# Gathers tied behind the gate products, an output product in split passes, and a softmax scaled late

## The chip, the cores and the metric

One core of a Trainium2 chip runs the whole program. The metric is device time in microseconds (us) of one execution, as the median over runs. The engines are TensorE (PE, matrix products and transposes), VectorE (DVE), ScalarE (ACT) and GpSimd (POOL); SyncE (SP) issues most of the loads. Each takes its instructions in order and waits on semaphores for the others.

## The reference

Four sub-layers on x of 512 tokens by 1024 channels, each with an RMS norm ahead of it, a shift, scale and gate from a conditioning vector (`ada`), and a residual:

```
y = rglru_block(h)              # layer 0: h @ w_in, a causal convolution of width 4, two gates,
                                # a linear recurrence over time, (gelu(gate) * hs) @ w_out
x = x + g1 * y;  x = x + g2 * peer(h)
y = mla_block(h, k, v)          # layer 1: 16 heads of softmax(q k) v, then @ w_o
x = x + g1 * y;  x = x + g2 * peer(h)

def peer(h):                    # per token: 8 heads, 16 experts each of 16384
    s = scores of two halves of the query against 128 sub-keys each; top 16 of both, top 16 of the 256 sums
    idx = e1 * 128 + e2;  g = softmax(top scores)
    act = gelu(h . u_tab[idx]);  return sum of g * act * v_tab[idx]
```

## The kernel before

Activations are channels on partitions by 512 tokens. Most products are split: an fp32 operand becomes a rounded high part (`hi`, ScalarE) and the rest (`lo`, VectorE, L163), and `mm3` (L187 to L189) makes three passes, hi x lo, lo x hi and hi x hi, into one PSUM bank. `outer` (L207) instead multiplies fp32 operands in one matmul. Weights come as `raw`, `wtile` splits them into `whi` and `wlo`.

A scheduler orders the instructions of each engine by its own estimate of when they can run; the source only sets priorities. `tc.issue_after(x)` is a hand on it: the instructions of its block stand behind x on the engine of x, with no wait added. The program has five stages by time: the recurrent block (0 to about 205 us), `peer` of layer 0 (to about 1522), attention (to about 1845), `peer` of layer 1 (to about 3158), a final norm.

The recurrent block (L335 to L454) makes the norm column `rcol` (L244), normalises and splits eight chunks, adds up the `rec` products, convolves them on VectorE (`xc`, L379), makes `gate` and the two recurrence gates, scans (L433), multiplies by the gelu (L436) and goes through `w_out` (`wo`, L207) in a loop over k, the last two k per output chunk. Products of the conditioning vector with a column block of its weight (`adas`, L151, one VectorE instruction of 128x1024 each) are strewn among it.

Attention (L537 to L725) takes the heads one by one: `scores` makes the products `s`, the mask and the maximum, the exponential (ScalarE, sums beside it), the reciprocal of the sums (L660) and four scalings of `p` (L662). `turn` transposes `p` on TensorE (`tp`, L670) and splits it, `context` multiplies with the values (`pv`) and copies the result into `ot`.

`peer` (L851 to L1090) serves three of the four token blocks (384 tokens) densely and the last by gathers. Dense: for every group of experts, `u_part` multiplies hidden states with a split `u` weight (24 matmuls 128x384), and the gate values are written out (`gact`, through `gscr`). In the gate stage 24 `gate_group`s (L821) build the weights of all experts for 16 tokens each: VectorE makes the one-hots `oo` (L835) and the products `pr` (L837) in two halves, TensorE multiplies them (`wps`, L843), ScalarE copies, a DMA writes `wscr`. `et` (L808) are transposed expert numbers, ready after decoding `e` (L800). Thirteen `u_part`s (`UDEC`) stand ahead of the groups, others between them, `UEND` = 5 behind the last. Then the value pass: 128 steps t, each 18 matmuls `acc` of `al`/`ah` with `vh`/`vl`; a step's weights `wt` are read back from `wscr` (`wfirst` serves t = 0 and 1).

The gathers (`gather_steps`, L1103) are 256 steps a layer: GpSimd issues an indirect DMA of 128 rows (`grow`, 512 KB, four buffers, L1113), then VectorE makes a dot product with `hn` (L1117, `gdot`) for u or adds the scaled row into `gacc` (L1122) for v, in turns of 16. How many steps are given out by when is counted by `done`: four in the loop over `UDEC`, 94 (`EARLY`) by the second last gate group, the others over the value pass.

Of the kernel before, what the change touches and what calls it, by code (L numbers as in the profile page):

```python
# [15 lines left out]
AF = mybir.ActivationFunctionType  # L16
OP = mybir.AluOpType
# [4 lines left out]
P = 128  # L22
D = 1024
KC = D // P
T = 512
# [21 lines left out]
UEND = 5  # L47
FIRST = 4
EARLY = 94
# [32 lines left out]
class Trunk:  # L82
# [157 lines left out]
    def rstd_row(self, n):  # L240
# [3 lines left out]
        nc.vector.reciprocal(col[:, 1], col[:, 0])  # L244
# [90 lines left out]
    def rglru(self):  # L335
        nc, io, tc = self.nc, self.io, self.tc
        with tc.tile_pool(name="lru", bufs=52) as pool, ExitStack() as st:
# [11 lines left out]
            with tc.tile_pool(name="ada", bufs=1) as early:  # L349
                ws, h = [], []  # L350
                for k in range(KC):
# [7 lines left out]
                    if k == 0:  # L359
                        outs = [self.bank("rec") for _ in range(KC)]  # L360
                    if k < KC - 2:
                        self.outer3(outs, ws, h, [k])
            late = st.enter_context(tc.tile_pool(name="lru2", bufs=10))
            s2, s4 = self.softplus_neg()
            hba, hbx = self.half_bias("ba"), self.half_bias("bx")
            xc, rec = [], []
            for m in range(KC):
# [6 lines left out]
                                     bias=self.vec("conv_b", m))  # L374
            win = [self.wtile(io["w_in"][m], KC, eng=nc.vector) for m in range(2)]
            for m in range(KC):
                a = xc[m]
                for s in range(1, 4):
                    nc.vector.scalar_tensor_tensor(a[:, s:], rec[m][:, :T - s], self.vec("conv_w", (3 - s) * KC + m),  # L379
                                                   a[:, s:], op0=OP.mult, op1=OP.add)  # L380
# [36 lines left out]
            for hd in range(4):  # L417
# [12 lines left out]
                for j in js:  # L430
# [8 lines left out]
                    ys.append(tt[j])  # L439
            self.todo = [*range(16, 40), *range(96, 112), *range(40, 96)]  # L440
            self.adas(12, late)
# [4 lines left out]
            for k in range(KC):  # L446
                ws.append(self.wraw(io["w_out"][k]))
                if k < KC - 2:
                    self.outer(outs, ws, ys, [k])
            self.preload(AF.Sqrt, last_gelu)  # L450
            for m in range(KC):
                self.outer(outs, ws, ys, range(KC - 2, KC), m)
# [84 lines left out]
    def mla(self):  # L537
        nc, io, tc = self.nc, self.io, self.tc
        with tc.tile_pool(name="mla", bufs=12) as pool, ExitStack() as st:
# [87 lines left out]
            att, ots, qts, pns, pts = [], {}, {}, {}, {}  # L627
# [17 lines left out]
            def scores(hd):  # L645
# [15 lines left out]
                for b, p in enumerate(pns[hd]):  # L661
                    nc.vector.tensor_scalar(p, p, st[:, 3, b:b + 1], None, op0=OP.mult)  # L662
# [12 lines left out]
            def context(hd):  # L675
                hp, s = divmod(hd, 2)
                if s == 0:
                    ots[hp] = pool.tile([P, T], F32, name="ot", tag="t")
                ops = self.bank("pv")
# [4 lines left out]
                nc.scalar.activation(ots[hp][64 * s:64 * s + 64], ops[:64], AF.Copy)  # L684
# [136 lines left out]
    def gate_group(self, pool, l, b, sg, et, gp):  # L821
# [5 lines left out]
        for t0 in range(0, TG, HT):  # L827
# [9 lines left out]
            nc.vector.tensor_tensor(pr.rearrange("p (q a) e t -> p q a e t", q=2), oo[:, 0:n4].unsqueeze(1).to_broadcast(two),  # L837
# [390 lines left out]
```

## Time and profile before

| | |
|---|---|
| median of 3 runs | 3173.54 us (3168.76 to 3174.25) |
| profiled execution | 3173.62 us, span 3171.8 us |
| mean granted clock of TensorE | 0.975 of full speed |
| busy: PE, DVE, ACT, POOL | 95%, 82%, 43%, 27% of the span |
| DMA | 821.13 MB, mean 259 GB/s |

The span is the profiled part of the execution. A row of a view of lines gives an engine, an operation with output and inputs, its shape, busy time, mean duration and what ended the idle time before it. TensorE is pipelined: one matmul's duration is longer than the distance between two starts. [...]

### The profile page before, as it was taken

Reading aid. Unit: us, or ns where it says so; the run is one execution under the profiler, and the core shown is the slowest. Engines: PE = TensorE matmul, PEld = TensorE weight load, DVE = VectorE, ACT = ScalarE, POOL = GpSimd, SP = SyncE. Lnnn points to the kernel's source line nnn. Section 1 sums busy time; section 2 is a strip of 40 time slices with the busy share of each in tenths; the row PEclk is TensorE's granted clock in tenths of the full one; section 3 lists DMA queues with packets and bytes.
Section 4 is the critical chain, followed back from the end, with each engine's and each line's share of the span. In section 5 each row is a group of like instructions: output and inputs, shape, how many; then the busy total and the mean of one; then the engine's idle time right before and its main releaser. Section 6 shows DMA issues by size and latency. Waiting matters only on the chain.

```text
span 3171.8 us, 43218 instructions
## 1 busy us (share of the span) xinstructions
PE 2997.4 (95%) x15334; PEld 2626.9 (83%) x15334; DVE 2585.5 (82%) x4927; ACT 1377.0 (43%) x1960; POOL 860.7 (27%) x653
## 2 busy tenths in 40 slices
PE   6999997999899999999889989989899899999997
PEld 5659997999777889998667679989899688889996
DVE  8859999988788888888578868998987677777886
ACT  5533245655334333333555642445555233333333
POOL 0000015433132214443356500034432211134440
PEclk9999998999999999999899999999999899999999
DMA  7444578999999999998113244478999999999994
GB/s 290 149 160 140 173 241 307 335 316 317 308 346 347 367 330 328 333 342 285 42 45 106 78 145 137 145 279 304 337 321 314 293 320 303 321 313 331 341 325 142
DMA packets 345111, 821.13 MB, mean 259 GB/s; under 512 B 33600, under 2 KB 179136, under 8 KB 338496
## 3 DMA queue, kind: packets, MB, share of 16 engines
q1 hardware_dynamic: 239632, 460.91, 43.5%
q0 software_dynamic: 73728, 268.47, 23.8%
q10 hardware_dynamic: 31536, 89.00, 7.4%
q8 instruction: 121, 1.98, 0.2%
q14 instruction: 94, 0.77, 0.1%
HBM read 730.98 MB, written 87.29 MB: 258 GB/s over the span
## 4 chain that ended last, share of the span: by engine, by line
PE 74%; DVE 11%; issue 6%; DMA 5%; ACT 2%; POOL 2%; DVEq 0%; SPq 0%; POOLq 0%; ACTq 0%
PE acc L187 10%; PE acc L188 10%; PE acc L189 10%; PE u L187 9%; PE u L188 9%; PE u L189 9%; PE wps L843 5%; PE pq L187 2%; PE pq L188 2%; PE pq L189 2%; DVE wlo L163 1%; PE wo L207 1%; DMA ada_raw<-in_adaw_dram 1%; DMA grow<-in_u_dram,idx 1%; DVE grow L1117 1%
## 5 line engine op out<-in xcount | busy, mean ns | idle before, releaser
L1113 POOL DMA_INDIRECT grow<-in_u_dram,idx x256 | 341.3, 1333 | 1317.3 <-DVE oh L791 702.8
L187 PE MATMUL u<-hh,wlo 128*128 128x384 f32 x2048 | 690.6, 337 | 1.6 <-DVE wlo L163 1.6
L189 PE MATMUL u<-hh,whi 128*128 128x384 f32 x2048 | 687.4, 336 | 0.0
L188 PE MATMUL u<-hl,whi 128*128 128x384 f32 x2048 | 685.7, 335 | 0.0
L187 PE MATMUL acc<-vh,al 128*128 128x512 f32 x1536 | 573.7, 392 | 33.4 <-DVE al L163 30.6
L188 PE MATMUL acc<-vl,ah 128*128 128x512 f32 x1536 | 601.4, 392 | 1.2 <-DVE vl L163 1.2
L189 PE MATMUL acc<-vh,ah 128*128 128x512 f32 x1536 | 601.2, 391 | 0.0
L1113 POOL DMA_INDIRECT grow<-in_v_dram,idx x256 | 352.4, 1376 | 750.5 <-DVE gacc L1122 439.8
L163 DVE TENSOR_TENSOR wlo<-raw,whi 128x1024 fp32r<-128x1024 f32 x307 | 373.1, 1216 | 110.9 <-ACT whi L162 110.7
L163 DVE TENSOR_TENSOR vl<-vraw,vh 128x1024 fp32r<-128x1024 f32 x256 | 313.2, 1223 | 165.5 <-ACT vh L162 164.8
L162 ACT ACTIVATE whi<-raw 128x1024 fp32r<-128x1024 f32 (+2 forms) x364 | 349.5, 961 | 104.5 <-PE acc L189 29.1
L187 PEld LDWEIGHTS u<-hh,wlo 128*128 128x128 f32 x2048 | 385.8, 188 | 5.2 <-issue 1.5
L188 PEld LDWEIGHTS u<-hl,whi 128*128 128x128 f32 x2048 | 385.1, 188 | 2.8
L189 PEld LDWEIGHTS u<-hh,whi 128*128 128x128 f32 x2048 | 384.8, 188 | 0.0
L187 PEld LDWEIGHTS acc<-vh,al 128*128 128x128 f32 x1536 | 289.5, 189 | 96.7 <-issue 23.8
L188 PEld LDWEIGHTS acc<-vl,ah 128*128 128x128 f32 x1536 | 289.9, 189 | 60.6 <-DVE vl L163 1.6
L189 PEld LDWEIGHTS acc<-vh,ah 128*128 128x128 f32 x1536 | 289.7, 189 | 60.7
L162 ACT ACTIVATE ah<-gact 128x384 fp32r<-128x384 f32 x240 | 125.9, 525 | 481.0 <-PE acc L189 282.3
L1122 DVE SCALAR_TENSOR_TENSOR gacc<-grow,gdot,gacc 128x1024 f32<-128x1024 f32 x254 | 324.8, 1279 | 9.8 <-DMA grow<-in_v_dram,idx 8.5
L1117 DVE CUSTOM_DVE_ANT_0 grow<-grow,hn 128x1024 f32<-128x1024 f32 x256 | 309.1, 1219 | 25.8 <-DMA grow<-in_u_dram,idx 25.6
L162 ACT ACTIVATE vh<-vraw 128x1024 fp32r<-128x1024 f32 x256 | 268.8, 1051 | 131.4 <-DMA vraw<-in_v_dram 48.9
L843 PE MATMUL wps<-pr,oo 128*128 128x128 f16 x1536 | 190.5, 297 | 31.8 <-DVE pr L837 31.8
(337 smaller groups left out, 4175.4 us busy)
## 6 DMA issues: line engine op xcount, KB each, us to landing
raw<-in_uT_dram SPq DMA_DIRECT2D x256, 512.0 KB, 5.4
vraw<-in_v_dram SPq DMA_DIRECT2D x256, 512.0 KB, 6.0
ada_raw<-in_adaw_dram SPq DMA_DIRECT2D x112, 512.0 KB, 4.5
wscr<-stg ACTq DMA_DIRECT2D x48, 1024.0 KB, 6.2
wt<-wscr SPq DMA_DIRECT2D x32, 1536.0 KB, 13.1
gscr<-gsp ACTq DMA_DIRECT2D x152, 192.0 KB, 4.9
gact<-gscr SPq DMA_DIRECT2D x152, 192.0 KB, 6.1
raw<-in_w_pq_dram SPq DMA_DIRECT2D x32, 512.0 KB, 3.6
```

Source lines behind the costliest of these rows:

```text
L162: nc.scalar.activation(hi, src, AF.Copy)
L163: return (eng or nc.vector).tensor_tensor(lo, src, hi.bitcast(F32), op=OP.subtract)
L187: nc.tensor.matmul(out, al, bh, start=first, stop=False)
L188: nc.tensor.matmul(out, ah, bl, start=False, stop=False)
L189: return nc.tensor.matmul(out, ah, bh, start=False, stop=last)
L207: self.nc.tensor.matmul(outs[m], ws[k][:, m, :], acts[k], start=k == 0, stop=k == KC - 1)
L843: last = nc.tensor.matmul(wps[:, t * P:t * P + P], oo[:, n4 + a, :, t], pr[:, q * n4 + a, :, t], start=q == 0, stop=q == 1)
L1113: nc.gpsimd.indirect_dma_start(out=row, out_offset=None, in_=tabs[s], in_offset=bass.IndirectOffsetOnAxis(ap=idx[:, k:k + 1], axis=0))
L1117: nc.vector.tensor_tensor_reduce(row, row, hn, op0=OP.mult, op1=OP.add, scale=1.0, scalar=0.0, accum_out=col)
L1122: nc.vector.scalar_tensor_tensor(acc, row, col, acc, op0=OP.mult, op1=OP.add)
```

## The change

It has four parts, and line numbers of the lines behind move by up to 14 (`pr` L850, dot products L1131, `gacc` L1136).

In `peer`, no gather steps are given out in the loop over `UDEC`. In the gate stage the steps of a turn are placed under `issue_after` of the last `pr` product of the group before, `EARLY` is 90 instead of 94, and it is reached by the group that is fourth from the end (`QUIET`) instead of second. `UEND` is 7: two more `u_part`s stand behind the last group.

In the recurrent block, `w_out` and the activations `ys` are split and `outer3` makes three passes (192 matmuls) in place of 64 fp32 ones. All but the first chunk's step and the softplus stand behind the norm's reciprocal; the first twelve `adas` stand behind the last convolution.

In attention the four scalings of `p` go. The reciprocals are transposed on TensorE into a bank `rr` (four transposes a head), and `ot` is multiplied by it after the copy.

```diff
@@ -44,9 +44,9 @@
-UEND = 5
-FIRST = 4
-EARLY = 94
+UEND = 7
+QUIET = 4
+EARLY = 90
@@ -241,7 +241,7 @@
-        nc.vector.reciprocal(col[:, 1], col[:, 0])
+        self.recip = nc.vector.reciprocal(col[:, 1], col[:, 0]).ins
@@ -348,7 +348,7 @@
-                for k in range(KC):
+                def step(k):
@@ -356,12 +356,16 @@
-                    if k == 0:
-                        outs = [self.bank("rec") for _ in range(KC)]
...
+                        if not outs:
+                            outs.extend(self.bank("rec") for _ in range(KC))
...
+
+                outs = []
+                for k in range(KC):
+                    with tc.issue_after(self.recip) if k else ExitStack():
+                        step(k)
...
-            s2, s4 = self.softplus_neg()
@@ -372,12 +376,14 @@
+            with tc.issue_after(self.recip):
+                s2, s4 = self.softplus_neg()
...
-                    nc.vector.scalar_tensor_tensor(a[:, s:], rec[m][:, :T - s], self.vec("conv_w", (3 - s) * KC + m),
-                                                   a[:, s:], op0=OP.mult, op1=OP.add)
+                    conv = nc.vector.scalar_tensor_tensor(a[:, s:], rec[m][:, :T - s], self.vec("conv_w", (3 - s) * KC + m),
+                                                          a[:, s:], op0=OP.mult, op1=OP.add).ins
@@ -436,20 +442,22 @@
-                    ys.append(tt[j])
+                    ys.append(self.pair(pool, "y"))
+                    self.split(ys[j][0], ys[j][1], tt[j])
...
-            self.adas(12, late)
+            with tc.issue_after(conv):
+                self.adas(12, late)
...
-                ws.append(self.wraw(io["w_out"][k]))
+                ws.append(self.wtile(io["w_out"][k], KC, eng=nc.vector))
...
-                    self.outer(outs, ws, ys, [k])
+                    self.outer3(outs, ws, ys, [k])
...
-                self.outer(outs, ws, ys, range(KC - 2, KC), m)
+                self.outer3(outs, ws, ys, range(KC - 2, KC), m)
@@ -624,7 +632,7 @@
-            att, ots, qts, pns, pts = [], {}, {}, {}, {}
+            att, ots, qts, pns, pts, norms = [], {}, {}, {}, {}, {}
@@ -658,8 +666,7 @@
-                for b, p in enumerate(pns[hd]):
-                    nc.vector.tensor_scalar(p, p, st[:, 3, b:b + 1], None, op0=OP.mult)
+                norms[hd] = st
@@ -676,12 +683,18 @@
+                rr = self.bank("rr")
+                st = norms.pop(hd)
+                for b in range(NB):
+                    nc.tensor.transpose(rr[:64, b * P:b * P + P], st[:, 3, b:b + 1].to_broadcast([P, 64]), self.ident)
...
-                nc.scalar.activation(ots[hp][64 * s:64 * s + 64], ops[:64], AF.Copy)
+                o = ots[hp][64 * s:64 * s + 64]
+                nc.scalar.activation(o, ops[:64], AF.Copy)
+                nc.vector.tensor_tensor(o, o, rr[:64], op=OP.mult)
@@ -834,8 +847,9 @@
-            nc.vector.tensor_tensor(pr.rearrange("p (q a) e t -> p q a e t", q=2), oo[:, 0:n4].unsqueeze(1).to_broadcast(two),
-                                    toks(gp).rearrange("p (q a) e t -> p q a e t", q=2), op=OP.mult)
+            prod = nc.vector.tensor_tensor(pr.rearrange("p (q a) e t -> p q a e t", q=2),
+                                           oo[:, 0:n4].unsqueeze(1).to_broadcast(two),
+                                           toks(gp).rearrange("p (q a) e t -> p q a e t", q=2), op=OP.mult)
@@ -846,7 +860,7 @@
-        return last.ins
+        return last.ins, prod.ins
@@ -957,24 +971,24 @@
-                    while done < FIRST * (i + 1) // UDEC:
-                        next(gsteps)
-                        done += 1
...
-                wlast = [None, None]
+                wlast, plast = [None, None], []
...
-                    wlast.append(self.gate_group(pool, l, i // nsg, i % nsg, *prep[i // nsg]))
+                    w, p = self.gate_group(pool, l, i // nsg, i % nsg, *prep[i // nsg])
+                    wlast.append(w)
+                    plast.append(p)
...
-                    while done < min(EARLY, FIRST + (EARLY - FIRST) * (i + 1) // (nt - 2)):
-                        next(gsteps)
-                        done += 1
+                    with tc.issue_after(plast[max(0, i - 1)]):
+                        while done < min(EARLY, EARLY * (i + 1) // (nt - QUIET)):
+                            next(gsteps)
+                            done += 1
```

Ahead of the first gate product, DVE, layer 0 (`gdot<-grow,hn` is a gather's dot product, `oo` and `pr` belong to the first gate group). Before:

```order
L835 TENSOR_TENSOR oo<-iota_e,et 128x2048 x2
L817 CAST gp<-gt 128x16x8
L780 TENSOR_REDUCE gsum<-g 128x8
L798 TENSOR_TENSOR oh<-oh 128x4x128
L1117 ISA grow,gdot<-grow,hn 128x1024
L1117 ISA gdot 128x1
L818 TENSOR_TENSOR gp<-gt,gp 128x16x8
L781 RECIPROCAL gsum<-gsum 128x8
L1117 ISA grow,gdot<-grow,hn 128x1024
L1117 ISA gdot 128x1
L798 TENSOR_TENSOR oh<-oh 128x4x64
L837 TENSOR_TENSOR pr<-oo,gp 128x2048 x2
```

With the change:

```order
L848 TENSOR_TENSOR oo<-iota_e,et 128x2048 x2
L813 TENSOR_TENSOR e_4610<-oh 128x64
L830 CAST gp<-gt 128x16x8
L793 TENSOR_REDUCE gsum<-g 128x8
L163 TENSOR_TENSOR wlo<-raw,whi 128x1024
L804 TENSOR_TENSOR oh<-iota_m,rc 128x1024
L831 TENSOR_TENSOR gp<-gt,gp 128x16x8
L794 RECIPROCAL gsum<-gsum 128x8
L808 TENSOR_TENSOR oh<-oh,ib 128x1024
L850 TENSOR_TENSOR pr<-oo,gp 128x2048 x2
L1131 ISA grow,gdot<-grow,hn 128x1024
L1131 ISA gdot 128x1
```

No dot product is left ahead of the first `pr`; the layer's first stands right behind it.

Start of the value pass, DVE, layer 0 (`gacc` are gathers of v, `al` the first step's weights, `x<-x,wt` the first product with weights that are read back). Before:

```order
L151 ISA ada_junk,mod<-ada_raw,csil,vecs 128x1024
L151 ISA mod 128x1
L1122 SCALAR_TENSOR_TENSOR gacc<-grow,gdot,gacc 128x1024 x2
L998 TENSOR_TENSOR x<-x,wfirst 128x384 x2
L1122 SCALAR_TENSOR_TENSOR gacc<-grow,gdot,gacc 128x1024 x2
L163 TENSOR_TENSOR al<-x,ah 128x384 x2
L151 ISA ada_junk,mod<-ada_raw,csil,vecs 128x1024
L151 ISA mod 128x1
L1122 SCALAR_TENSOR_TENSOR gacc<-grow,gdot,gacc 128x1024
L471 CAST ps_a<-ps_pi 128x512
```

With the change:

```order
L1012 TENSOR_TENSOR x<-x,wfirst 128x384 x2
L151 ISA ada_junk,mod<-ada_raw,csil,vecs 128x1024
L151 ISA mod 128x1
L163 TENSOR_TENSOR vl<-vraw,vh 128x1024
L1136 SCALAR_TENSOR_TENSOR gacc<-grow,gdot,gacc 128x1024 x4
L151 ISA ada_junk,mod<-ada_raw,csil,vecs 128x1024
L151 ISA mod 128x1
L163 TENSOR_TENSOR al<-x,ah 128x384 x2
L1136 SCALAR_TENSOR_TENSOR gacc<-grow,gdot,gacc 128x1024 x4
L163 TENSOR_TENSOR vl<-vraw,vh 128x1024
L1012 TENSOR_TENSOR x<-x,wt 128x384 x3
L163 TENSOR_TENSOR al<-x,ah 128x384 x2
```

Four gathers stand ahead of the first `al` in one piece and four more behind it, ahead of the `wt` product, where one stood.

End of the recurrent block, DVE (`tanh<-tanh,gate` are the activations that go into `w_out`, `yl` their low parts, `wlo` the low parts of its rows among others, `x<-wo` the residuals). Before:

```order
L151 ISA mod 128x1
L436 TENSOR_TENSOR tanh<-tanh,gate 128x512
L433 SCALAR_TENSOR_TENSOR tanh<-a,tanh 128x512
L151 ISA ada_junk,mod<-ada_raw,csil,vecs 128x1024
L151 ISA mod 128x1
L436 TENSOR_TENSOR tanh<-tanh,gate 128x512
L278 SCALAR_TENSOR_TENSOR gs_f_1370<-mod,vecs 128x8
L163 TENSOR_TENSOR wlo<-raw,whi 128x1024
L282 SCALAR_TENSOR_TENSOR x<-wo,mod,x 128x512
L163 TENSOR_TENSOR wlo<-raw,whi 128x1024
L282 SCALAR_TENSOR_TENSOR x<-wo,mod,x 128x512
L163 TENSOR_TENSOR wlo<-raw,whi 128x1024
```

With the change:

```order
L439 SCALAR_TENSOR_TENSOR tanh<-a,tanh 128x512
L438 TENSOR_TENSOR tanh<-tanh,g 128x512
L163 TENSOR_TENSOR wlo<-raw,whi 128x1024
L163 TENSOR_TENSOR yl<-tanh,yh 128x512
L442 TENSOR_TENSOR tanh<-tanh,gate 128x512
L163 TENSOR_TENSOR yl<-tanh,yh 128x512
L439 SCALAR_TENSOR_TENSOR tanh<-a,tanh 128x512
L163 TENSOR_TENSOR yl<-tanh,yh 128x512
L442 TENSOR_TENSOR tanh<-tanh,gate 128x512
L163 TENSOR_TENSOR yl<-tanh,yh 128x512
L163 TENSOR_TENSOR wlo<-raw,whi 128x1024 x2
L282 SCALAR_TENSOR_TENSOR x<-wo,mod,x 128x512 x3
```

The last products of `w_out` wait for `yl` and `wlo` rows, which before were not there for `w_out`; the residual follows them.

## Rows read from the trace of the kernel before

**Rows 1.** The waits of TensorE over the span, from the line that waits to the line waited for: total us, times, longest us.

```profile
PE wps L843 <- DVE pr L837: 31.8, 8, 9.9
PE tp L670 <- DVE p L662: 13.9, 12, 3.0
PE et L808 <- DMA raw<-in_uT_dram: 8.0, 1, 8.0
PE gate L187 <- DVE wlo L163: 5.8, 1, 5.8
PE et L808 <- DVE e L800: 2.4, 1, 2.4
```

**Rows 2.** Timeline of TensorE, 483 to 503 us: start, duration, instruction, [idle before it <- what ended it].

```profile
492.50 0.48 PE L808 MATMUL et<-ident,e 128*128 128x128 f32 x1 [8.01 <-DMA raw<-in_uT_dram]
502.15 1.10 PE L843 MATMUL wps<-pr,oo 128*128 128x128 f16 x8 [8.96 <-DVE pr L837]
```

**Rows 3.** Timeline of VectorE, 470 to 504 us, same columns.

```profile
492.23 0.21 DVE L800 TENSOR_TENSOR e<-oh 128x64 f32<-128x64 bf16 x1
499.57 1.18 DVE L1117 CUSTOM_DVE_ANT_0 grow<-grow,hn 128x1024 f32<-128x1024 f32 x1
500.88 2.35 DVE L837 TENSOR_TENSOR pr<-oo,gp 128x2048 f16<-128x2048 f16 x2
```

**Rows 4.** The table of stretches behind four pauses: stretch, its length, busy time of PE, PEld, DVE, ACT and POOL (instructions), granted clock, DMA share, GB/s.

```profile
502.00:505.60 3.60, 3.45 (x30) 3.45 (x30) 3.60 (x8) 2.30 (x3) 1.52 (x2) 0.51 0.82 251
2136.50:2140.60 4.10, 4.04 (x33) 4.04 (x33) 4.01 (x8) 2.88 (x3) 0.94 (x1) 0.51 0.57 192
2242.90:2249.70 6.80, 3.07 (x27) 3.07 (x28) 6.80 (x13) 1.92 (x3) 3.24 (x3) 0.50 1.02 339
608.00:611.40 3.40, 3.40 (x26) 3.40 (x24) 3.40 (x5) 3.40 (x4) 0.87 (x1) 0.50 1.08 399
```

**Rows 5.** Waits of VectorE for gathered rows of u in two stretches, 440 to 830 us (layer 0) and 2080 to 2490 us (layer 1): total us, times, longest.

```profile
DVE grow L1117 <- DMA grow<-in_u_dram,idx: 6.3, 4, 3.8
DVE grow L1117 <- DMA grow<-in_u_dram,idx: 5.0, 5, 3.6
```

**Rows 6.** The list of DMA issues, 2215 to 2250 us: count, median us from issue to landing.

```profile
grow<-in_u_dram,idx POOLq DMA_INDIRECT x12, 8.0
```

**Rows 7.** Timelines at the start of the value pass of layer 1: TensorE, SyncE's queue, VectorE.

```profile
2468.68 0.76 PE L187 MATMUL acc<-vh,al 128*128 128x512 f32 x1 [10.20 <-DVE al L163]
2464.22 8.25 SPq L993 DMA_DIRECT2D wt<-wscr  x2
2478.35 1.03 DVE L998 TENSOR_TENSOR x<-x,wt 128x384 f32<-128x384 f32 x2 [9.30 <-DMA wt<-wscr]
```

**Rows 8.** The table of stretches, two pieces of the value passes of layers 0 and 1, columns as in rows 4.

```profile
950.00:1050.00 100.00, 97.86 (x428) 79.69 (x427) 81.25 (x112) 38.80 (x52) 24.75 (x17) 1.00 1.01 353
2500.00:2600.00 100.00, 100.00 (x443) 82.82 (x442) 74.63 (x106) 35.41 (x48) 14.99 (x16) 1.00 0.92 306
```

**Rows 9.** Timeline of VectorE among the convolutions, a `wlo` and an ada product.

```profile
79.94 1.22 DVE L163 TENSOR_TENSOR wlo<-raw,whi 128x1024 fp32r<-128x1024 f32 x1
82.39 1.27 DVE L151 CUSTOM_DVE_ANT_0 ada_junk<-ada_raw,csil,vecs 128x1024 bf16<-128x1024 f32 x1
```

**Rows 10.** TensorE by lines, 140 to 210 us (busy us, mean ns | idle before), and its timeline at the end of the recurrent product (first and last of 21).

```profile
L207 PE MATMUL wo<-tanh,raw 128*128 128x512 f32 x128 | 55.1, 592 | 0.0
65.04 0.39 PE L187 MATMUL rec<-hmh,wlo 128*128 128x512 f32 x1
69.58 0.39 PE L189 MATMUL rec<-hmh,whi 128*128 128x512 f32 x1
```

**Rows 11.** The table of stretches for 80 to 200 us, columns as in rows 4.

```profile
80.00:200.00 120.00, 118.79 (x351) 67.98 (x352) 89.95 (x138) 57.61 (x79) 0.00 (x0) 0.98 0.49 162
```

**Rows 12.** Attention: the scalings by lines over 1594 to 1846 us, timelines of VectorE, GpSimd and TensorE, and a stretch behind a pause (columns as in rows 4).

```profile
L662 DVE TENSOR_SCALAR p<-p,st 128x512 f32<-128x512 f32 x64 | 51.5, 864 | 0.5
1703.03 3.49 DVE L662 TENSOR_SCALAR p<-p,st 128x512 f32<-128x512 f32 x4
1715.02 1.76 DVE L662 TENSOR_SCALAR p<-p,st 128x512 f32<-128x512 f32 x3
1704.39 1.45 POOL L163 TENSOR_TENSOR qt<-qf,qt 96x512 fp32r<-96x512 f32 x1
1616.20 1.03 PE L670 MATMUL tp<-ident,p 128*128 128x128 f32 x8
1703.60:1710.40 6.80, 6.51 (x19) 5.28 (x20) 5.19 (x11) 1.57 (x3) 4.38 (x4) 0.50 0.15 48
```

**Rows 13.** Timeline of GpSimd, issues of gathered rows, 499 to 612 us: the first and the last of 29, and two between.

```profile
499.61 1.95 POOL L1113 DMA_INDIRECT grow<-in_v_dram,idx  x1 [2.40 <-DVE gp L818]
...
534.05 4.48 POOL L1113 DMA_INDIRECT grow<-in_v_dram,idx  x1 [5.79 <-DVE gacc L1122]
539.18 0.94 POOL L1113 DMA_INDIRECT grow<-in_v_dram,idx  x1 [0.65 <-DVE oh L798]
...
610.53 1.88 POOL L1113 DMA_INDIRECT grow<-in_u_dram,idx  x1 [4.21 <-DVE g L782]
```

**Rows 14.** Timeline of VectorE, 533.5 to 541 us.

```profile
540.61 1.22 DVE L835 TENSOR_TENSOR oo<-iota_e,et 128x2048 f16<-128x2048 f16 x1 [1.49 <-PE wps L843]
```

**Rows 15.** The gate products of layer 0, one tile's view: count, shortest, median and longest ns, first and last start.

```profile
L843 PE MATMUL wps<-pr,oo x768: 278/298/305, 502.1 to 799.4; 128*128 128x128 f16 x192
```

## The prediction

> **What bounds the kernel now.** I read the waits of TensorE first: TensorE is busy for most of the span, so what it waits for is what an edit can give back. Five of its waits are touched by the change [rows 1]: 31.8 us before the gate products `wps` for `pr`, 8.0 and 2.4 us before the transposes `et`, 13.9 us before the attention transposes `tp` for the scaled `p`, 5.8 us before a `gate` product of the recurrent block. Next I read the timeline at the largest of them. In layer 0 TensorE stands 8.01 us before `et` and 8.96 us before the first `wps` [rows 2]. VectorE shows who is late: `e` comes at 492.23, `pr` begins at 500.88, and gather rows' dot products of 1.18 us stand between [rows 3]. The first pause is put down to a DMA, but `et` starts as `e` ends, so VectorE is what TensorE waits for. The order of VectorE has 15 such dot products ahead of the first `pr` in either layer. [...]
>
> **The gate groups.** The change puts every dot product behind the `pr` of the group before; the new order has none ahead of the first `pr`. Fifteen at 1.18 us are 18 us of VectorE, about the two pauses of layer 0 (8.01 + 8.96 = 17.0) and more than layer 1's (2.4 + 9.9 = 12.3). I take these 29.3 us as gone; what is left of the list, 42.2 − 29.3 = 12.9 us, lies at later groups and has the same cause, `pr` behind dot products, so I count it too. [...] Together 49.2 us.
>
> Against it stands the tie itself. VectorE is in order, so a row that is not there when its turn comes holds `wlo`, `oo` and `pr` behind it, and TensorE after them. Today such waits are 6.3 us in layer 0 and 5.0 in layer 1 [rows 5]. The rows used to have a head start of 15 ahead of the first group and now have none; groups 2 to 5 carry 16 dot products instead of 10. Four row buffers are refilled in rounds of an issue on GpSimd, a landing of 8.0 us [rows 6] and a dot product. No row shows the new waits. Below, they are zero, or even negative by today's 11.3 us; above, they are what the first rival prices. I double today's: −11.3 us. The gates then give 49.2 − 11.3 = 38 us (range 14 to 49). Two `u` parts more behind the last group are work moved, not added: 48 matmuls on TensorE either way, and their loads move with them.
>
> **The start of the value pass.** In layer 1 TensorE waits 10.20 us for the first `al`, and then t = 2 needs `wt`, which is issued at 2464.22 and read at 2478.35 after a wait of 9.30 us [rows 7]. The issue follows the write of the last `u` part's activations, so more parts behind the last group do not bring it forward. What the first pause gives up, the second takes: zero, with the 10 us of one pause as a bound upward. In the new order the same path has ten to twelve gathers between the last `pr` and the first `al`, and three or four more ahead of the first `wt` product; a late round of rows there is the bound downward, −10 us.
>
> In the value pass eleven gathers more are left (80 done at its start, not 91), and by t = 84 eight of them are caught up. In layer 0 the DMA engines are full there (share 1.01 at 353 GB/s), in layer 1 not (0.92) [rows 8]. Eight rows of 0.52 MB at 353 GB/s are 11.9 us of transfer in layer 0 alone; TensorE was at 97.9 us of 100 in that stretch, so most of a small surplus is hidden. I take −3 us (0 to −12).
>
> **The recurrent block.** Three things pull forward. The first normalised chunk loses one ada product (1.27 us) and one `wlo` (1.22 us) ahead of it [rows 9]: 2.5 us. The pause of 5.8 us before the second gate product falls by the ada products that stood between the convolutions, two at 1.27 us: 2.5 us. The output product is 55.1 us for 128 records of 64 fp32 matmuls; three split passes are 192 matmuls at the pitch of the recurrent product, 21 of them from 65.04 to 69.58, 20 pitches, 0.227 us each [rows 10]: 43.6 us, so 11.5 less. The sum is 16.5 us, if TensorE alone counted. But VectorE has only 30.0 us idle of the 120 from 80 to 200 us (89.95 busy) [rows 11], and the change puts into it eight `wlo` at 1.22, eight `yl` (half the width, so 0.7 at most) and twelve ada products at 1.27 that used to lie earlier: 9.8 + 5.6 + 15.2 = 30.6 us. That fills it. The last `yl` then comes near 180 to 195 us with the output passes of the last chunks behind it, and TensorE waits for most of what it saved. I take 5 us; bounds −3 (VectorE late by its overflow and a wait more) and +16.5. Eight more ScalarE copies lie beside, ScalarE being busy half of that stretch (57.61 of 120).
>
> **Attention.** Out go 64 scalings with a mean of 0.864 us, 51.5 us of VectorE in all [rows 12], and the 13.9 us that TensorE waits for them; the transposes then wait for the exponential, a step earlier. In come 64 small transposes on TensorE: eight `tp` take 1.03 us, so 64 x 0.129 = 8.2 us, all on the path, and 16 products of 64x512, the size class of the scaling: 14 us of VectorE at most, 0.7 of them at the tail behind the last head. One of the half-clock stretches starts after such a wait, with 6.51 us of work [rows 12]; I take back 3. So 13.9 − 8.2 − 0.7 + 3 = 8 us (0 to 16).
>
> Among these rows four scalings take 3.49 us beside a GpSimd split, three take 1.76 with GpSimd idle: 0.87 against 0.59 each. [...]
>
> **Sum.** 38 + 0 − 3 + 5 + 8 = 48 us. The profiled execution took 3173.62 us (span 3171.8), the median is 3173.54, so 3173.6 − 48 = **3126 us**. About 0.2%, 6 us, is what a measurement of this kernel can tell from no change.
>
> **Rivals.**
>
> *Rows come late in the first groups* (chance 0.18). For: from 499.61 to 610.53 GpSimd issues 29 rows, one per 3.96 us, and one issue takes 4.48 us where another takes 0.94 [rows 13]; the long one lies under unbroken VectorE work, the short one in a pause of 1.49 us [rows 14]. VectorE gets fuller, so long issues become common. The 24 groups' products run from 502.1 to 799.4 [rows 15]. Two `u` parts leave this stretch, 48 matmuls of 384 columns, an estimate of 8.2 us at three quarters of 0.227 each; (297.3 − 8.2) / 24 = 12.0 us a group. Sixteen rows at 3.96 us are 63.4 us, four groups 48.0: 15.4 us in each layer, 31 in place of 11.3. That gives 3146 us. Against: today's pace is mostly that of demand, since the long pauses of GpSimd end with a buffer that VectorE frees. [...]
>
> *The value pass of layer 0 becomes DMA-bound* (0.08): the full 11.9 us in place of 3, 3135 us. For: a share of 1.01. Against: TensorE at 97.9%.
>
> *More comes back* (0.13): the rows keep up (5 of the 11.3), VectorE keeps pace in the output passes (5), and half of one pause at the value pass goes (5): 3111 us. For it speaks that VectorE idles 30 us in the recurrent block; against, the fixed path over `wt`.
>
> *Slower: the rows' pace sets the gate stage* (0.06). All 72 dot products of the 24 groups stand in order on VectorE. At a pace p per row a layer's stage lasts 72p; it exceeds the 24 x 12.0 = 289 us of the groups from p = 4.01, and eats the rest of the gain (48 + 11.3 over two layers, 30 each) from p = 4.43 us. At 4.48 us, the long issue, for every row: 322.6 − 289 = 34 us a layer, 3126 − 11 + 68 = 3183 us. For: today's 3.96 us lies just below the first of these points. Against: it is demand that sets it, as above, and rounds of four that overlap (an issue of 0.94, a landing of 8.0, a dot product) give 2.5 us a row.
>
> *The edits cancel or do not act* (0.03): 3173 us. Against: the order shows the dot products behind `pr`.
>
> **Numbers.** The forecast has 0.52; its own range is 3112 to 3140. Faster holds 0.52 + 0.18 + 0.08 + 0.13 = 0.91, of which I move 0.02 to the middle, for terms that all end at their lower bounds; so faster 0.89, same 0.03 + 0.02 = 0.05, slower 0.06. The range that keeps 8 in 10 reaches from the case that gives more to beyond the late rows, with the terms' other bounds for part of it: **3107 to 3152**.
>
> **What would show it.** Right: no wait above 3 us before the first `et` and `wps` of either layer, granted clock 1.0 there; no wait `tp` for `p`; `wo` passes with pauses for `yl`. Wrong: VectorE waits for `grow` far above 22 us in the gates; `wps` waits for `pr` still near 30 us; DMA share at 1.0 with TensorE below 97% after the value pass starts in layer 0; the recurrent block ending after 204 us.

## The result, and the profile after

The changed kernel takes 3154.87 us (median of 6 runs, 3150.46 to 3157.25) against 3172.91 us of the kernel before, run beside it; the ratio is 0.9946 with a 95% interval of 0.9934 to 0.9959. It is faster by 18 us, not by 48: outside the range of 3107 to 3152. The profiled execution has a span of 3151.9 us.

The stages, from the first and last starts and ends of their products in the tile views of both traces (us; "queries" are the first `pq` products of a layer, "attention" goes from its first product, `lat`, to them; some 39 us of norms and of the end of the program are in no row):

| stretch | before | after | difference | forecast |
|---|---|---|---|---|
| start to queries, layer 0 | 210.8 | 215.4 | +4.6 | −5 |
| queries to last `u` product, layer 0 | 609.7 | 597.0 | −12.7 | half of −38 |
| pause, layer 0 | 12.4 | 11.1 | −1.3 | 0 |
| value pass, layer 0 | 684.1 | 697.7 | +13.6 | +3 |
| attention | 318.7 | 307.6 | −11.1 | −8 |
| queries to last `u` product, layer 1 | 607.0 | 595.4 | −11.6 | half of −38 |
| pause and value pass, layer 1 | 690.3 | 688.7 | −1.6 | 0 |

The waits of TensorE after the change (total us, times, longest):

```profile
PE acc L187 <- DVE al L163: 30.6, 8, 11.1
PE wps L857 <- DVE pr L850: 15.2, 7, 3.9
PE acc L187 <- ACT vh L162: 9.6, 5, 4.3
PE wo L187 <- ACT yh L162: 8.3, 1, 8.3
PE u L187 <- ACT gsp L909: 3.0, 2, 1.5
PE tp L677 <- ACT p L667: 1.1, 4, 0.6
```

Beside [rows 1]: `et` is gone from the list, `wps` for `pr` is halved, `tp` waits no longer for the scaling. New are 8.3 us for `yh` (the high part of an activation that goes into `w_out`) and 3.0 for `gsp` (gate values on their way out); the waits for `vh`, the high part of a row block of v, rose from 2.6 to 9.6. Both pauses of [rows 2] are gone: the first `wps` starts at 486.35 us right behind a `u` product. The next group has a pause of 2.99 us:

```profile
501.62 1.58 PE L857 MATMUL wps<-pr,oo 128*128 128x128 f16 x12 [2.99 <-DVE pr L850]
```

The clock behind it and behind five other pauses of the gate stages, of 3.92 (at 696.70 us), 1.36, 2.48, 2.04 and 1.97 us (columns as in [rows 4]):

```profile
501.60:505.30 3.70, 3.45 (x29) 3.17 (x29) 3.52 (x5) 2.31 (x3) 0.83 (x2) 0.54 1.05 410
696.60:700.00 3.40, 3.31 (x29) 3.31 (x30) 3.40 (x4) 2.15 (x3) 0.76 (x1) 0.55 1.01 367
532.40:535.80 3.40, 3.40 (x12) 3.40 (x11) 3.40 (x7) 1.32 (x3) 1.68 (x1) 0.50 1.03 422
2133.20:2136.60 3.40, 3.40 (x24) 3.40 (x23) 3.40 (x5) 3.40 (x4) 1.68 (x1) 0.51 0.70 239
2222.00:2225.40 3.40, 3.40 (x21) 3.40 (x19) 3.40 (x6) 2.69 (x3) 1.83 (x1) 0.50 0.80 255
2324.40:2327.80 3.40, 3.40 (x31) 3.40 (x30) 3.40 (x4) 2.46 (x3) 2.82 (x1) 0.50 0.99 277
```

Behind a pause of 2.99 us lies as much work at a granted clock of about 0.5 as behind the one of 8.96: 3.45 us here (0.54) and 3.45 in [rows 4] (0.51). Six such stretches hold 20.4 us of work, where the four of [rows 4] held 14.0. VectorE's waits for gathered rows of u, as in [rows 5], are now (440 to 830 us, then 2080 to 2490):

```profile
DVE grow L1131 <- DMA grow<-in_u_dram,idx: 1.1, 2, 0.8
DVE grow L1131 <- DMA grow<-in_u_dram,idx: 4.0, 1, 4.0
```

They fell. In the value pass of layer 0 one stretch tells most (the kernel before, then the kernel after; to be read with [rows 8]):

```profile
900.00:1000.00 100.00, 96.37 (x419) 77.98 (x418) 82.08 (x124) 38.08 (x49) 29.95 (x22) 1.00 1.02 370
900.00:1000.00 100.00, 90.00 (x375) 72.88 (x374) 78.67 (x117) 32.05 (x43) 40.08 (x27) 0.95 0.98 351
```

### The profile page after: what moved, and what is told of

The parts are those of the page before. It is cut to its first block, busy times and chain, and to the rows that moved or that the text cites. A ratio compares the mean times of both kernels' runs of the same rounds, so it can differ in the third digit from the quotient of the medians.

```text
span 3151.9 us, 43413 instructions
## 1 busy us (share of the span) xinstructions
PE 2996.1 (95%) x15462; PEld 2651.3 (84%) x15462; DVE 2571.8 (82%) x4895; ACT 1387.8 (44%) x1974; POOL 854.5 (27%) x653
## 4 chain that ended last, share of the span: by engine, by line
PE 55%; DVE 6%; DMA 2%; ACT 2%; issue 2%; POOL 1%; DVEq 0%; SPq 0%; POOLq 0%; ACTq 0%
PE acc L188 8%; PE acc L187 8%; PE acc L189 8%; PE u L187 7%; PE u L189 7%; PE u L188 7%; PE wps L857 3%; DMA vraw<-in_v_dram 1%; PE pq L187 1%; PE pq L188 1%; PE pq L189 1%; ACT p L667 1%; DVE vl L163 1%; DVE ada_junk L151 1%; DVE p L662 1%
## 5 line engine op out<-in xcount | busy, mean ns | idle before, releaser
L187 PE MATMUL acc<-vh,al 128*128 128x512 f32 x1536 | 570.3, 393 | 40.2 <-DVE al L163 30.6
L163 DVE TENSOR_TENSOR wlo<-raw,whi 128x1024 fp32r<-128x1024 f32 x315 | 383.3, 1218 | 113.2 <-ACT whi L162 111.5
L162 ACT ACTIVATE whi<-raw 128x1024 fp32r<-128x1024 f32 (+2 forms) x372 | 358.3, 964 | 143.4 <-PE acc L189 30.4
L1136 DVE SCALAR_TENSOR_TENSOR gacc<-grow,gdot,gacc 128x1024 f32<-128x1024 f32 x254 | 324.9, 1279 | 17.2 <-DMA grow<-in_v_dram,idx 16.0
L1131 DVE CUSTOM_DVE_ANT_0 grow<-grow,hn 128x1024 f32<-128x1024 f32 x256 | 309.3, 1219 | 9.2 <-DMA grow<-in_u_dram,idx 8.9
L860 ACT ACTIVATE stg<-wps 128x512 f32<-128x512 f32 x192 | 187.3, 1108 | 54.7 <-PE wps L857 46.2
```

Source lines behind the costliest of these rows:

```text
L162: nc.scalar.activation(hi, src, AF.Copy)
L163: return (eng or nc.vector).tensor_tensor(lo, src, hi.bitcast(F32), op=OP.subtract)
L187: nc.tensor.matmul(out, al, bh, start=first, stop=False)
L860: nc.scalar.activation(stg[:, :, c:c + 4].rearrange("p e t -> p t e"), wps.rearrange("p (t e) -> p t e", t=4), AF.Copy, scale=1.0 / GSCALE)
L1131: nc.vector.tensor_tensor_reduce(row, row, hn, op0=OP.mult, op1=OP.add, scale=1.0, scalar=0.0, accum_out=col)
L1136: nc.vector.scalar_tensor_tensor(acc, row, col, acc, op0=OP.mult, op1=OP.add)
```

## The experiments

Twelve kernels ran. "Before" was run beside each; ratios are to it, with 95% intervals.

| run | median us | ratio |
|---|---|---|
| tie_alone | 3157.44 | 0.9951 [0.9934, 0.9968] |
| late_scaling_alone | 3161.59 | 0.9966 [0.9956, 0.9976] |
| split_alone | 3178.96 | 1.0023 [1.0012, 1.0033] |
| order_alone | 3169.24 | 0.9991 [0.9981, 1.0000] |
| no_split | 3148.98 | 0.9924 [0.9911, 0.9938] |
| early_94 | 3157.80 | 0.9952 [0.9937, 0.9967] |
| ada_no_load | 3163.18 | 0.9971 [0.9960, 0.9982] |
| uend_5 | 3146.60 | 0.9923 [0.9908, 0.9938] |
| spread_ada | 3145.48 | 0.9913 [0.9896, 0.9929] |
| before_spread_ada | 3168.53 | 0.9981 [0.9971, 0.9990] |
| short_ada | 3137.40 | 0.9881 [0.9864, 0.9897] |
| combined | 3130.44 | 0.9868 [0.9851, 0.9884] |

### The four parts alone

**tie_alone**: of the change only `UEND`, `QUIET`, `EARLY` and the tie in `peer`.

> The kernel before with the gather part alone (tie, EARLY, QUIET, UEND). Theory 1 (each part acts by itself): the gate stages of both layers give some 12 us each as in the whole change, the value pass of layer 0 loses some 11 us as there, so 3158 to 3162 us. Theory 2 (the loss in layer 0's value pass comes from the moved work of another part, the times of the recurrent block shifting it): the gate stages give 24 us, nothing is lost, about 3149 us.

Measured 14.6 us less than before. Queries to last `u` product: −11.7 us in layer 0, −13.5 in layer 1. The value pass of layer 0: 699.1 us, +15.0. Theory 1 holds: the loss comes with the gather part.

**late_scaling_alone**: of the change only the lines of attention.

> The kernel before with the late softmax scaling alone. Theory 1: attention gives 11 us as in the whole change, no TensorE wait for p, 3162 us; recurrent block and both peers as before to 1 us. Theory 2 (part of the 11 us came from other state that the first layer handed over): 3167 us or more.

Measured 10.5 us less; attention 308.9 us, −9.8. Theory 1. (Where attention is unchanged, the same stretch varies by 3.4 us over the kernels.)

**split_alone**: of the change only

```diff
-                    ys.append(tt[j])
+                    ys.append(self.pair(pool, "y"))
+                    self.split(ys[j][0], ys[j][1], tt[j])
...
-                ws.append(self.wraw(io["w_out"][k]))
+                ws.append(self.wtile(io["w_out"][k], KC, eng=nc.vector))
```

and `outer3` in place of `outer`.

> The kernel before with w_out and ys in split passes alone, the order of the recurrent block's ada products and softplus as before. Theory A (the split is what makes the recurrent block longer: yh, yl and wlo queue on ScalarE and VectorE): the block ends 5 to 7 us later, 3178 us. Theory B (the order edits make it longer, the split shortens TensorE's work by 11 us): the block ends 4 to 8 us earlier, 3167 us.

Measured 6.9 us more; the queries begin at 215.9 us instead of 210.8. Theory A. The stages behind move too, though no line of them was edited: queries to last `u` product take 5.8 and 9.4 us more, pause and value pass 7.9 and 6.6 less.

**order_alone**: of the change only the `issue_after` lines of the recurrent block.

> The kernel before with the order edits of the recurrent block alone (steps and softplus behind the reciprocal, twelve ada products behind the convolutions), w_out in fp32. Theory A (the split hurts): the start and the gate pause give 3 to 6 us, 3168 us. Theory B (the order edits hurt, the ada products land where VectorE feeds ScalarE and TensorE): 5 to 10 us longer, 3180 us.

Measured 2.8 us less, at the edge of what shows; the queries begin at 206.2 us, 4.6 earlier. Theory A, if weakly. The four differences, −14.6 − 10.5 + 6.9 − 2.8, add to −21.0 us; together the parts gave −18.

### What the split costs, and why

**no_split**: the whole change with `wraw` and `outer` for `w_out` as before.

> The whole change without the split of w_out (fp32 output product as before): tie, late scaling and order edits. Theory 1 (the parts add, the split costs its 7 us): 3172 - 14.6 - 10.5 - 2.8 = 3144 us, 10 us under the whole change. Theory 2 (the split is harmful only with the old order of ada products): 3154 us as the whole change.

3148.98 us, halfway between the two forecasts, and the intervals of this ratio and of the whole change's barely overlap. The queries decide for theory 1: they begin at 207.1 us instead of 215.4, and 6 us of the 7 come back (3154.87 against 3148.98).

**short_ada**: the whole change, and

```diff
-                self.adas(12, late)
+                self.adas(12, late, width=64)
```

twice, 64 columns instead of 1024 for the last 24 ada products of the block.

> The whole change, with the last 24 ada products of the recurrent block made over 64 columns instead of 1024 (their results are partial): some 27 us of VectorE less in it, loads unchanged. Theory V (VectorE's work delays the fifth activation, and TensorE waits for it with the split passes): the fifth product with the gate comes by 168 us instead of 177, the pause of 8.3 us before its passes falls under 2, the queries start at 206 us or sooner instead of 215. Theory A (ScalarE's order and table loads set it): the pause stays at 6 us or more.

The fifth product with the gate (the first of the second four), and the first `wo` product behind the pause. After, whole change: VectorE, ScalarE, TensorE.

```profile
177.45 1.29 DVE L442 TENSOR_TENSOR tanh<-tanh,gate 128x512 f32<-128x512 f32 x2
180.88 1.13 ACT L162 ACTIVATE yh<-tanh 128x512 fp32r<-128x512 f32 x2
181.55 2.07 PE L187 MATMUL wo<-yh,wlo 128*128 128x512 f32 x4 [8.27 <-ACT yh L162]
```

short_ada: VectorE, TensorE.

```profile
168.47 1.89 DVE L442 TENSOR_TENSOR tanh<-tanh,gate 128x512 f32<-128x512 f32 x3
163.75 0.50 PE L187 MATMUL wo<-yh,wlo 128*128 128x512 f32 x1 [1.95 <-DVE wlo L163]
```

With VectorE relieved the fifth activation comes 9 us earlier, the pause of 8.27 us is gone (1.95 us before another product), and the queries begin at 202.9 us, 12.5 earlier than in the whole change. Theory V: VectorE sets that pause. It is not the whole of the delay: without the split the fifth activation stood at 160.1 us (no_split), 8.4 earlier than here, with all ada products in full.

### Where layer 0's gain went

**early_94**:

```diff
-QUIET = 4
-EARLY = 90
+QUIET = 2
+EARLY = 94
```

> The whole change with EARLY = 94 and QUIET = 2 again, the tie kept. Theory R (layer 0's value pass is longer since fewer gathers are done at its start and are caught up where the DMA engines are full): TensorE idles about 7 us there instead of 16, the pass is 8 us shorter, the gate stages lose up to 4 us each, 3150 to 3154 us. Theory S (the loss comes from which load stands where in SyncE's queue and one late row, not from the number): the pass stays within 3 us of the whole change's 698 us.

3157.80 us; value pass 701.7 us, TensorE idle 18.2 us in it. Theory R falls: four more rows given out ahead change neither the gate stages (596.6 and 595.3 us) nor the loss. Theory S had the pass within 3 us of 698; it is 4 longer than in the whole change.

**ada_no_load**: `self.adas(1, stop=68, raw=hn)` in the value pass of layer 0.

> The whole change, and the 23 ada products in layer 0's value pass read a tile that is there already instead of loading 0.5 MB each: 12 MB less for the DMA engines, the same VectorE work (those columns of the modulation are not the reference's). Theory D (the pass is longer because the DMA engines are full in its first 280 us): TensorE idles under 5 us in it instead of 16, the pass falls from 698 to 684 us or less, the whole to 3141 us or less. Theory S (one late row and the order of the queue): idle stays above 10 us.

The pass fell to 681.5 us, TensorE's idle time in it to 4.9 us, near what theory D says (684 or less, under 5). The whole did not become shorter, 3163.18 us, through something that I had not foreseen: with no load to wait for, the scheduler moved the ada products ahead of the gate groups. VectorE by lines, 215 to 480 us, and TensorE's timeline in this run:

```profile
L152 DVE CUSTOM_DVE_ANT_0 ada_junk<-hn,csil,vecs 128x1024 bf16<-128x1024 f32 x13 | 16.7, 1283 | 0.0
```

```profile
496.11 0.48 PE L822 MATMUL et<-ident,e 128*128 128x128 f32 x1 [9.13 <-DVE e L814]
505.32 0.47 PE L822 MATMUL et<-ident,e 128*128 128x128 f32 x1 [8.74 <-DVE e L814]
```

Thirteen of them, 17 us of VectorE, lie there, and by 500 us all 24 (the expectation has 23) are done, ahead of the first `wps`. Two pauses of the size of [rows 2] are back, both before `et`, with 5.52 us more before the first `wps`. It shows by accident what the first step of the prediction said, and makes the run weak evidence for the value pass, which began 28 us later and had lost the products' VectorE work as well as their loads.

**spread_ada** and **before_spread_ada**, the whole change and the kernel before with

```diff
-                if t % 3 == 2 and l == 0:
+                if t % 5 == 4 and l == 0:
```

> The whole change, but the 23 ada products of layer 0's value pass come every fifth step instead of every third, so their 12 MB are asked for over 115 steps, not 70. Theory D (layer 0 from the gate stage to about step 70 is bound by the DMA engines, so that what the gate stage gains the value pass pays back): TensorE idles 4 to 8 us in the pass instead of 16, the pass 684 to 690 us instead of 698, the whole 3141 to 3148 us. Theory S (a late row and the order of the queue): the idle time stays above 12 us, 3152 us or more.

> The kernel before with the same spreading alone. Theory D: there the pass is only at the edge, TensorE's 7.4 us of idle time in it fall to about 4, 3168 us; the difference between this and the kernel with the whole change and the spreading is 24 us or more, where it is 18 without it. Theory S: 3172 us, and a difference of 18 as before.

With the change: 3145.48 us, the pass 689.1 us, idle 10.3 us (of these 7.1 at its start). On the kernel before: 3168.53, the pass 679.2. The same stretch of [rows 8]'s pass in spread_ada and then in before_spread_ada:

```profile
900.00:1000.00 100.00, 96.79 (x419) 79.18 (x418) 82.10 (x120) 36.34 (x48) 34.68 (x25) 0.98 1.01 364
```

```profile
900.00:1000.00 100.00, 100.00 (x441) 82.49 (x440) 82.31 (x121) 39.23 (x52) 23.15 (x19) 1.00 1.04 363
```

The DMA engines are as full as in the whole change (1.01, there 0.98), but TensorE is held up less, 96.79 us busy instead of 90.00. Both gains are clear of noise. The difference that the change makes is 23 us where it was 18, less than the 24 of theory D, and the intervals do not tell 23 from 18. So theory D, with the idle time at 10 rather than 4 to 8 us. Spreading moves VectorE work too: 12 ada products stand between 823 and 1110 us instead of 19, 9 us less of VectorE, which was busy for 82% of that stretch in the whole change. No run separates the two.

The strongest reading comes from all runs together. From the first queries to the end of the value pass, layer 0 takes:

| kernels | us |
|---|---|
| before, after, tie_alone, late_scaling_alone | 1306.2, 1305.8, 1308.1, 1308.8 |
| split_alone, order_alone, no_split, early_94, uend_5, short_ada | 1304.1, 1309.1, 1306.4, 1309.6, 1305.3, 1304.5 |
| ada_no_load (with the pauses that it brought back) | 1317.2 |
| before_spread_ada, spread_ada, combined | 1300.1, 1296.6, 1292.5 |

The ten kernels of the first two lines, whose stretches to the last `u` product differ by 23 us (592.2 to 615.5), end the pass within 5.5 us of each other: what the gate stage gains, the pass pays back. Only the runs with later ada loads make it shorter. Layer 1, which has no such loads, keeps the change's gain (−11.6 and −1.6). The sum alone does not say what binds. The DMA share is 0.90 and 0.89 from 440 us to the last `u` product, before and after, and 1.00 and 0.98 from 820 to 1110 us; so the engines are full in the first 290 us of the pass, and not quite ahead of it. And in split_alone TensorE idles only 4.2 us in the pass: its 1304.1 us are TensorE's own time.

### The two parts behind the last group

**uend_5**:

```diff
-UEND = 7
+UEND = 5
```

> The whole change with UEND = 5: two u parts less behind the last gate group. Theory 1 (moved work, no effect on the sum): 3153 to 3157 us, the tail 21 us instead of 31, the groups' stretch longer by the same 8 to 10 us. Theory 2 (the longer tail is what hides gathers ahead of the value pass): the first al comes later after the last u part, 20 us instead of 11, 3162 us.

3146.60 us, 8 less than the whole change: neither theory. (The two intervals overlap by a little; the stretches below show where the time went.) TensorE's waits in it for `pr`, 440 to 830 us, then 2080 to 2450 us:

```profile
PE wps L857 <- DVE pr L850: 5.0, 2, 3.7
PE wps L857 <- DVE pr L850: 3.2, 2, 2.9
```

8.2 us instead of 15.2. Two stretches at a granted clock of about 0.5 are left in the gate stages, not six:

```profile
501.90:505.30 3.40, 3.18 (x27) 2.90 (x27) 3.40 (x6) 2.13 (x3) 0.65 (x1) 0.51 1.04 416
2130.10:2133.50 3.40, 3.40 (x27) 3.40 (x26) 3.40 (x5) 3.37 (x4) 1.68 (x1) 0.50 0.83 296
```

In layer 1 the stretch of the groups' products is 299.7 us with `UEND` = 5 and 295.4 with 7, 4.3 shorter, but the tail behind it grew from 20.8 to 31.0, 10.2 longer (1.5 of it the new wait for `gsp`). Queries to last `u` product are 592.2 and 589.5 us: −17.5 in either layer against before. Layer 0 paid its part back: the value pass took 704.2 us, 6.5 more than in the whole change.

**combined**: no_split, `UEND` = 5 and the spread ada products together.

> The whole change without the split of w_out, with UEND = 5 and the ada products every fifth step. If the parts add: 3149 (without the split) - 8 (UEND) - 8 to 12 (spreading) = 3129 to 3133 us, under both kernels. If layer 0 is bound by its loads from the gate stage on whatever is done, 3140 us.

3130.44 us, faster than both kernels by more than their intervals: the parts add.

## Why the prediction was wrong, step by step

**The tie: right, and against my first rival.** The waits of [rows 1] that it was to end were 42.2 us. With `UEND` = 5 the gate stages gave 35.0 us, near the 38 of the sum, though not by its terms: 8.2 us of the waits remain (42.2 − 8.2 = 34.0), and the new row waits of 11.3 us did not come. VectorE's waits for rows of u fell from 11.3 to 5.1 us in the whole change and to 7.9 with `UEND` = 5. So rows were not late, and issues on GpSimd took as long as before: over the span a mean of 1.35 us for rows of u and 1.37 for rows of v, against 1.33 and 1.38. (The last rival counted 72 dot products in the groups; in layer 0 after the change 40 are that and 31 additions of rows of v, and no term rests on it.) The 49.2 us of the gates have 7.0 us for the clock in them, half of the 14.0 us of work in [rows 4]; this was my estimate, and no run shows it. Of the 116 matmuls in that work 112 are `wps`, and 32 `wps` take 3.94 us at 0.50 (2136.56 us, before) and 3.95 at 1.00 (540.56 us, after). Only the four `u` matmuls lose; `u` matmuls start 0.32 us apart at 0.50 (532.69 to 535.25 us, after) and 0.17 at 1.00 (536.20 to 540.21). Nor did such stretches go: in the whole change pauses down to a sixth of the 8.96 us of [rows 2] are followed by as much work at a granted clock of about 0.5, and there are more of them, 20.4 us of work in place of 14.0. With `UEND` = 5 it is 6.6 us.

**The two `u` parts: wrong.** I costed them at nothing: "work moved, not added". The step looked only at TensorE's matmuls. In the gate stage those parts fill time in which VectorE makes the next `pr`; taken out, they shorten the groups' stretch by only 4.3 us, while the waits for `pr` rise from 8.2 to 15.2 us, and the tail gains 10.2. That is 5 to 6 us in each layer, and 24.3 us of gate stages where 38 were forecast.

**The value pass of layer 0: mechanism named, size wrong.** The rival "becomes DMA-bound" had 11.9 us and 0.08; the pass lost 13.6. My price counted eight late rows, and early_94 shows that the number of rows left is not the cause. What the runs show in its place: TensorE comes to the pass earlier and waits there, where the DMA engines are full (0.98 from 820 to 1110 us), and the sum stays near 1306 us. [rows 8] had shown the share at 1.01, and I read TensorE's 97.9% as slack. Of the 13.6 us, 8.2 are TensorE standing idle (7.8 us before, 16.0 after), and 10.2 us of the pass behind the pauses at 913 and 980 us are at 0.50 of the clock. `acc` matmuls start 0.43 us apart there (915.21 to 917.34) and 0.23 at 1.00 (918.38 to 920.88), so about 4.8 of these 10.2 us are lost, most of the rest. The two longest waits inside the pass, 3.19 us at 947.13 and 4.26 at 980.43, are for `vh`, and ScalarE, which makes it, stands for the load of v:

```profile
946.02 1.06 ACT L162 ACTIVATE vh<-vraw 128x1024 fp32r<-128x1024 f32 x1 [9.17 <-DMA vraw<-in_v_dram]
979.32 1.06 ACT L162 ACTIVATE vh<-vraw 128x1024 fp32r<-128x1024 f32 x1 [5.80 <-DMA vraw<-in_v_dram]
```

The wait of 2.55 us at 913.48 has another cause, a late row at 909.46 us, where VectorE waits 6.19 us and everything behind it; the DMA share from 900 to 913 us is 0.64, so these engines were not full there. How the 13.6 us divide between transfers, late rows and the order of the loads stays open:

```profile
909.46 1.28 DVE L1136 SCALAR_TENSOR_TENSOR gacc<-grow,gdot,gacc 128x1024 f32<-128x1024 f32 x1 [6.19 <-DMA grow<-in_v_dram,idx]
```

**The recurrent block: sign wrong.** I said that VectorE's idle 30.0 us [rows 11] would be filled by 30.6 us, and took +5 of the 16.5 us. The effect was mis-sized in two places. In the output product the 11.5 us saved are lost whole: the fifth activation comes at 177.45 us, where no_split has 160.1, and behind it the split needs four chunks of 24 passes, 21.8 us at 0.227 [rows 10], with 8.27 us of waiting ahead and 6.05 us of work at 0.50 of the clock behind. From its first to its last matmul `wo` takes 55.1 us, as long as the fp32 products, which were slower but never waited. And `wo` begins at 151.36 us, 11.7 later than in no_split. There I had named ScalarE's eight more copies and let them go, since ScalarE was half busy. But in ScalarE's order in this kernel two waits for VectorE, of 6.95 and 3.29 us, lie ahead of the parts of the gates that TensorE needs; no_split has neither pause of TensorE, and its clock there is 1.00 (ScalarE, TensorE, and the stretch):

```profile
126.05 0.72 ACT L435 ACTIVATE tanh<-tanh,tiny 128x512 f32<-128x512 f32 x1 [6.95 <-DVE a L416]
136.55 0.63 ACT L162 ACTIVATE yh<-tanh 128x512 fp32r<-128x512 f32 x1 [3.29 <-DVE tanh L442]
130.81 3.78 PE L403 MATMUL ri<-xc,raw 128*128 128x512 f32 x4 [3.31 <-ACT gate L393]
137.81 0.79 PE L187 MATMUL gate<-hmh,wlo 128*128 128x512 f32 x1 [3.22 <-ACT g L405]
129.60:143.30 13.70, 9.27 (x17) 5.50 (x18) 12.35 (x20) 10.35 (x17) 0.00 (x0) 0.50 0.48 152
```

Which of VectorE's load and ScalarE's order is to blame for these two pauses no run separates; in short_ada the first is left (3.19 us) and the second gone. The order edits alone took away the pause of 5.8 us and end `wo` 8.9 us earlier than before; the norm behind it then keeps TensorE 5.85 us instead of 2.56, so the queries come 4.6 us earlier, near the 5 forecast, of which 2.8 show in the whole.

**Attention: right, with the clock's part too small.** −11.1 us, and −10.5 alone, where 8 were forecast (0 to 16). The waits for `p` fell from 13.9 to 1.1 us. Among the heads, work at 0.50 of the clock fell from 19.4 to 6.8 us, worth 5.9 by an estimate at the ratio of the `acc` matmuls above, where I took back 3. GpSimd is not idle beside all three scalings of 1.76 us in [rows 12]: two of its splits (`wlo`) run from 1715.64 to 1717.38 us; the first scaling takes 0.49 us, the third, beside them, 0.96. With the scalings gone, GpSimd's own splits moved both ways: the mean `wlo` of 128x256 fell from 0.92 to 0.83 us, the mean `qt` rose from 1.43 to 1.54, and TensorE's waits for `wlo` of GpSimd before `wo` rose from 0.4 to 5.4 us.

**The start of the value pass: right,** −1.3 and −1.0 us against 0; a second wait stayed, 4.22 us before and 3.88 after in layer 1.

In sum: 48 − 13.7 (gates, the two parts above all) − 10.6 (value pass) − 9.6 (recurrent block) + 3.1 (attention) + 2.3 (pauses) + 0.6 (the rest) = 20 us, the difference of the spans (19.9).

## What to carry to other kernels

Ask of each stretch which resource is full over all of it, and follow a gain into the next stretch: where the DMA engines are at 1, as in the first 290 us of this value pass (1.00 before, 0.98 after), time won ahead can be waited for there. Filler work for TensorE between products that wait for VectorE can be worth much of its own length, here 5 to 6 of the 10 us that two parts take; moving it behind the last of them is not free. An engine that is half busy can still set the pace if what others need lies behind its waits, as behind the 6.95 and 3.29 us of ScalarE here (busy for 63.01 us from 80 to 200 us). And a faster form of a product can be worth nothing if the engine that feeds it comes late and the product then waits: `wo` takes 55.1 us in either form, with VectorE busy for 101.71 of the same 120 us and a wait of 8.27 us.

## What the runs showed of the hardware

Six pauses of 1.36 to 3.92 us of TensorE in the gate stages are followed by as much work at a granted clock of about 0.5 as a pause of 9 us: 3.45 us of work at 0.54 behind 2.99 us, 3.40 at 0.50 in the stretch behind 1.36, 3.45 at 0.51 behind 8.96 [rows 4]. Not every pause is: behind the 3.19 us at 947.13 in the value pass of layer 0 the clock stays at 1.00.

```profile
947.00:951.00 4.00, 3.87 (x17) 3.22 (x18) 3.89 (x6) 2.16 (x4) 0.78 (x1) 1.00 1.03 398
```

What a granted clock of 0.50 costs differs by product: starts 0.32 us apart instead of 0.17 for `u`, 0.43 instead of 0.23 for `acc`, and 32 `wps` in 3.94 us instead of 3.95.

Twelve megabytes of loads, with their 24 VectorE products, asked for over 115 steps instead of 70 gave 9 us in the changed kernel at a DMA share of 1.01 where it was 0.98 (900 to 1000 us).
